# A diffusion backbone step on one core: negated weight copies put directly behind their rounding, dots spread differently

## The chip, the cores and the metric

The kernel runs on one core of one Trainium2 chip. The metric is the device time of one execution in microseconds. The engines are named as the profile names them: PE (matrix engine, PEld its weight loads), DVE (vector engine), ACT (scalar engine), POOL (GpSimd, here a queue that issues transfers), SP (a queue that issues most of the loads).

## What is computed

The reference is one inference step of a backbone of two layers over T = 640 tokens (512 latent ones and 128 of context) of D = 1024 features, in float32. Layer 0 mixes tokens by a bidirectional state-space scan, layer 1 by differential attention; after each mixer stands a gated convolutional channel mixer (called FFN below). Each part is normalised, shifted, scaled and gated by a linear map of a conditioning vector:

```python
def modulation(cvec, w, b):
    m = jax.nn.silu(cvec) @ w + b
    return jnp.split(m[:, None, :], 6, axis=-1)

def conv_ffn(h, up_w, conv_w, conv_b, down_w):
    u = dwconv(h @ up_w, conv_w, conv_b)
    a, v = jnp.split(u, 2, axis=-1)
    return (jax.nn.silu(a) * v) @ down_w
...
        xp = xp + p_g1 * op
        xs = xs + s_g1 * os_
        ffn_p = (ffn_up_w[i], ffn_conv_w[i], ffn_conv_b[i], ffn_down_w[i])
        xp = xp + p_g2 * conv_ffn(modulate(xp, norm_ffn_g[i], p_sh2, p_sc2), *ffn_p)
        xs = xs + s_g2 * conv_ffn(modulate(xs, norm_ffn_g[i], s_sh2, s_sc2), *ffn_p)
```

The hidden width of the FFN is 2816, that is 22 tiles of 128 rows in each of its two halves.

## The kernel before

Every large product is made of three products of rounded numbers: a matrix is split into a rounded high part and a low part, the rest, and hi·hi, hi·lo and lo·hi are added up. So each weight needs a high tile `whi` and a low tile `wlo`. Weights come in numbered *units*: `prefetch` (L157) has SP load `raw<u>`, up to 512 KB (128 x 1024), and `cast` (L169) makes whi and wlo. There are three ways: most units have whi copied by ACT and wlo subtracted by DVE; units whose `kind` is a tuple are sums of two weights, `s0` to `s3`, made by DVE, copied by ACT and subtracted by DVE; and units in the set `summed` (nearly all loads of the up weights that need no sum) get a second ACT copy with the sign turned, minus the rounded weight, after which POOL issues a transfer that adds the weight from memory into wlo (L202 to L204). The last way takes no DVE time, but the low part is there only when the transfer has landed.

An FFN (L695) takes the 22 tiles of the hidden width in pairs: tile p of one half with tile p of the other. The first pairs (6 in layer 0, 4 in layer 1, `S0`) are two plain tiles each. The others (`pair8`, L794) are computed with seven block products in place of eight. A block is 12 matmuls into one bank; X, V and Y are the banks of one pair. X is written by the first block (`begin7`, L779), copied out by ACT as `uraw`, and then gets more blocks on top; V is copied out as `p5`. Four units belong to a pair: wa, two of sums, and wv; in the layer-0 FFN, units 77 to 80 belong to pair 6, the first of the kind, 81 to 84 to the next. What ends a pair is `epilogue` (L712): a convolution of both halves on ACT and DVE (tiles `ca` and `cv`), their gated product cv, its rounded copy `mh` and its low part `ml`, made like wlo with a negated copy and a POOL transfer.

The pairs go in five groups (`SUB`): after a group, `project_out` (L344) multiplies the finished tiles by down weights into tiles `po`; ACT copies these out as `y`, and a POOL transfer adds y to the residual in memory (`xd`). The last group of six goes through `project_last` (L359), which adds to the residual in SBUF (`xr`) and takes the squares for the next norm.

Beside this runs a task that computes layer 1's modulation, `mod_rest` (L660). It has 48 tiles; each is a load of 512 KB (`mw`, issued by SP, two buffers) and two DVE instructions of 128 x 1024 (L674, the *dots*), outputs `junk` and mw. A task is advanced by `hook`, called after every second step of matmuls; `self.gap` says how many hooks pass from a dot to the next, and each dot is held until the matmul issued last before it has run. Which tiles are done where is set by `DOTS = 3, 36, 48`: tiles 0 to 2 in layer 0's mixer output (there the loads are called `ew`), 3 to 35 in layer 0's FFN, 36 to 47 in the attention.

The order on each engine's queue is made by a scheduler from data dependences and priorities, roughly the order of the program; what stands in `tc.high_priority()` is put ahead of what does not. In `pair8` the copies `uraw` and `p5` and the additions to uraw stand in it.

Of the kernel before, what the change touches and what calls it, by code (L numbers as in the profile page):

```python
# [11 lines left out]
BF16 = mybir.dt.bfloat16  # L12
I32 = mybir.dt.int32
AF = mybir.ActivationFunctionType
ALU = mybir.AluOpType
# [21 lines left out]
SUB = (0, 4), (4, 8), (8, 12), (12, 16), (16, 22)  # L37
# [3 lines left out]
RAW = 4  # L41
NS = 4
S0 = 6, 4
DOTS = 3, 36, 48
TH = T // 2
ATT_SPLIT = 6
NF = 11
# [3 lines left out]
class Step:  # L51
# [117 lines left out]
    def cast(self, upto):  # L169
        while len(self.wcast) <= min(upto, len(self.units) - 1):  # L170
            u = len(self.wcast)
            self.prefetch(u)
            n = self.units[u][1]
            r = self.wraw[u]
            kind = self.units[u][2]
            place = self.units[u][3] or ("x" if self.px and u % 5 > 2 else "w")
            wp, t, b = (self.pw, "w", 3) if place == "w" else (self.px, "x", 2)
            hi = wp.tile([P, 1024], F32R, tag=t + "hi", name=f"whi{u}", bufs=b)
            lo = wp.tile([P, 1024], F32R, tag=t + "lo", name=f"wlo{u}", bufs=b) if u else None
            if u == 0:  # L180
                half = lambda t, j: t.rearrange("p (k j m) -> p k j m", k=KT, j=2)[:, :, j, :]
                r3 = r[:, :n].rearrange("p (k m) -> p k m", k=KT)
                self.act(half(hi, 0), r3, AF.Copy)
                self.tt(half(hi, 1), r3, half(hi, 0).bitcast(F32), ALU.subtract)
            elif isinstance(kind, tuple):
                ns, j0, ia, iv = kind
                self.prefetch(u + iv)
                ra, rv = self.wraw[u + ia], self.wraw[u + iv]
                w = ns * P
                for j in range(j0, j0 + 1024 // w):  # L190
                    x = self.slot("f", f"s{j}", bufs=NF)[:, :w]
                    a, b, op = ((rv[:, :w], rv[:, w:2 * w], ALU.add), (self.s.get(0), ra[:, :w], ALU.subtract),
                                (ra[:, :w], rv[:, :w], ALU.subtract), (ra[:, w:2 * w], self.s.get(1), ALU.subtract))[j]
                    self.tt(x, a, b, op)
                    self.s[j] = x
                    c = slice(w * (j - j0), w * (j - j0 + 1))
                    self.act(hi[:, c], x, AF.Copy)
                    self.tt(lo[:, c], x, hi[:, c].bitcast(F32), ALU.subtract)
            else:
                c = slice(kind or 0, n)  # L200
                self.act(hi[:, c], r[:, c], AF.Copy)
                if u in self.summed:  # L202
                    self.act(lo[:, c], r[:, c], AF.Copy, scale=-1.0)
                    self.nc.gpsimd.dma_start(lo[:, c], self.units[u][0][:, c], accum_op=ALU.add)  # L204
                else:
                    self.tt(lo[:, c], r[:, c], hi[:, c].bitcast(F32), ALU.subtract)
            self.wcast[u] = (hi, lo)

# [486 lines left out]
    def ffn(self, l, h, nextnorm, pool):  # L695
# [3 lines left out]
        mid = {}  # L699
# [131 lines left out]
        def pair(p, more):  # L831
            if p >= S0[l]:
                if p == S0[l]:
                    self.drain(self.seven)
                    finish_operands()
                return pair8(p, more)
            ua = copy_out(self.next_tile(h, "up"))
            epilogue(p, ua, copy_out(self.next_tile(h, "up")))

        self.start_tiles(h)  # L840
        done = 0
# [6 lines left out]
        with self.tc.tile_pool(name=f"sums{l}", bufs=1, side="right", reuse_waits="tile") as tp:  # L848
            self.seven = self.add(operands(sevens, tp), 1)
            for s, (k0, k1) in enumerate(SUB):  # L850
                while done < min(k1 + 1, FT):
                    if not l and done == 3:
                        junk = lambda: self.slot("sq", "junk", BF16, cols=1024, bufs=1)
                        self.modtask = self.add(self.mod_rest(1, *DOTS[:2], self.cb, self.mod_row, junk), 1)
                    self.gap, self.rest = 3 if done < S0[0] else 9, 0
                    pair(done, done + 1 < min(k1 + 1, FT))
                    done += 1
                if s < len(SUB) - 1:
                    self.gap = 4
                    if self.modtask:  # L860
                        self.modtask[1] = self.ticks + 1
                    self.project_out(mid, range(k0, k1), self.gate(l, 1),
                                     to=lambda i: self.slot("y", "y", bufs=3, pool=pool) if l
                                     else self.slot("f", "y", bufs=NF) if i % 2 else self.tmp("y"))
# [1 line left out]
            self.drain(self.modtask)  # L866
            self.modtask = None
        self.restore()
        self.project_last(mid, range(*SUB[-1]), self.gate(l, 1), nextnorm, parts="CD" if l else "AB", save=not l)


    def ssd_consts(self, pool):
# [266 lines left out]
    def ssd(self, h, dtps, nextnorm, pool):  # L1139
        xf = [[None] * 4 for _ in range(4)]  # L1140
        zs = [[] for _ in range(4)]
        bcs, scanned, gt = [None] * 4, [False] * 4, [None] * 4

        def finish(g):

            yield from self.ssd_group(g, xf[g], *bcs[g], pool)
            scanned[g] = True
            while len(zs[g]) < 4:
                yield 1
            for t in range(4):  # L1150
                self.stt(xf[g][t], xf[g][t], 0.5, zs[g][t], ALU.mult, ALU.mult)
            yield 1
            yield from self.ssd_norm(g, xf[g], pool)

        def z_tiles(g):
            for t in range(4):
                ps = self.next_tile(h, "z")
                z = self.slot("f", f"z{g}{t}", bufs=NF)
                self.act(z, ps[:, PO:PO + T], AF.Tanh, scale=0.5)
                self.stt(z, z, 1.0, ps[:, PO:PO + T], ALU.add, ALU.mult)  # L1160
                zs[g].append(z)

        tmod = self.add(self.mod_rows(1, pool, 7))
        tdt = self.add(self.ssd_dt(dtps))
        self._advance(tdt)
        for g in range(4):
            for t in range(4):
                ps = self.next_tile(h, "x")
                xf[g][t] = self.xslot(f"xf{g}{t}") if g < 2 else self.slot("f", f"xf{g}{t}", bufs=NF)
                self.ssd_xbc(ps, 4 * g + t, xf[g][t])  # L1170
            bc = []
            for j in (16, 20):
                ps = self.next_tile(h, "bc")
                o = self.slot("bc", f"bc{g}{j}", bufs=3, pool=pool)
                self.ssd_xbc(ps, j + g, o)
                bc.append(o)
            if g == 0:
                self.drain(tmod)
                self.drain(tdt)
            else:  # L1180
                z_tiles(g - 1)
                while not scanned[g - 1]:
                    self._advance(gt[g - 1])
            bcs[g] = bc
            gt[g] = self.add(finish(g), 2)
        z_tiles(3)
        self.drain(gt[0])
        self.drain(gt[1])
        hy = [self.split(xf[i // 4][i % 4], f"y{i}") for i in range(8)]
        self.x = []  # L1190
        for i in range(KT):
            xi = self.xslot(f"xr{i}")
            self.nc.sync.dma_start(xi, self.a["xT"][i])
            self.x.append(xi)
        self.project_out(hy, range(8), self.gate(0, 0))
        self.drain(gt[2])
        self.drain(gt[3])
        hy = [self.split(xf[2 + i // 4][i % 4], f"y{8 + i}") for i in range(8)]
        self.modtask = self.add(self.mod_rows(2, pool, 7))
        row = lambda: pool.tile([P, 1024], F32, tag="rb", name="ew", bufs=3)  # L1200
        junk = lambda: self.slot("t", "junk", BF16, cols=1024, bufs=4)
        self.gap, self.rest = 4, 3
        early = self.add(self.mod_rest(1, 0, DOTS[0], self.cond_rows(row), row, junk), 8)
        self.project_last(hy, range(8), self.gate(0, 0), nextnorm, save=True, before=[early])


# [199 lines left out]
    def heads(self, h, nextnorm, pool):  # L1406
# [7 lines left out]
        next(consts, None)  # L1414
        junk = lambda: pool.tile([P, 1024], BF16, tag="junk", name="junk", bufs=1)
        self.gap, self.rest = 6, 0
        dots = self.add(self.mod_rest(1, *DOTS[1:], self.cb, self.mod_row, junk), 10)
        for hd in range(8):
            q, qp = self.att_evac(self.next_tile(h, "q"), hd, "q", pool)
            k, kp = self.att_evac(self.next_tile(h, "k"), hd, "k", pool)  # L1420
# [36 lines left out]
    def weight_units(self):  # L1457
# [9 lines left out]
        def ffn(l):  # L1467
# [13 lines left out]
            return out  # L1481

        u = [(*x, None, None) for x in u] + ffn(0)
        v, u = u, []
        for hd in range(8):
# [155 lines left out]
```

## Time and profile before

| | us |
|---|---|
| median of 3 runs | 1855.98 (1850.47 to 1857.3) |
| the profiled execution | 1847.69 |
| its span, first to last instruction | 1845.9 |
| PE busy | 1782.4 (97%) |
| DVE busy | 1465.1 (79%) |
| ACT busy | 1166.3 (63%) |
| POOL busy | 153.4 (8%) |

Times in rows are counted from the span's start. Layer 0's FFN lies at about 567 to 1018, with its first seven-product pair at 676 and projections near 725, 804, 884 and from 985 on; the attention begins after it, and layer 1's FFN lies in the stretch 1400 to 1780. A row of an engine's timeline has the start, the duration, the engine, the line, the operation, out<-in, the shape, and in brackets how long the engine had been idle and what ended that. A row of PE's waits has the total, how often, and the longest.

### The profile page before, as it was taken

The numbers are of one execution on the slowest core, as the hardware profiler recorded it, in microseconds if no ns is written. First come the engines' busy times: TensorE is split into PE (matmuls) and PEld (weight loads), VectorE is DVE, ScalarE is ACT, GpSimd is POOL, SyncE is SP. The second block draws the span as 40 slices with busy tenths as digits, with TensorE's granted clock in tenths as the row PEclk, the third lists the DMA queues.
The fourth block names the chain that finished last, engine by engine and source line by source line (L and its number), as shares of the span: only waits on it lengthen the run. The fifth ranks groups of instructions, "written<-read, shape, count | busy, mean of one in ns | idle before, by whom it ended". The sixth has DMA issues, their size and how long they took to land.

```text
span 1845.9 us, 33794 instructions
## 1 busy us (share of the span) xinstructions
PE 1782.4 (97%) x12914; PEld 1684.1 (91%) x12914; DVE 1465.1 (79%) x2907; ACT 1166.3 (63%) x2329; POOL 153.4 (8%) x180
## 2 busy tenths in 40 slices
PE   7999999999999999999999989999999999999996
PEld 5899999999989999999999888888899999999996
DVE  5689999999858968879776788888878856758584
ACT  3489686879426656667574556566636666767661
POOL 0000000000000121212210000000000122122210
PEclk9999999999999999999999999999999999999998
DMA  9844353446655697988966222223134587787871
GB/s 344 259 133 139 99 148 105 120 142 196 213 178 160 168 239 175 228 214 190 233 154 217 88 85 82 88 83 113 48 126 116 120 167 176 155 182 157 173 196 58
DMA packets 116990, 289.13 MB, mean 157 GB/s; under 512 B 13422, under 2 KB 20186, under 8 KB 116828
## 3 DMA queue, kind: packets, MB, share of 16 engines
q1 hardware_dynamic: 90908, 223.92, 37.2%
q0 software_dynamic: 25344, 62.53, 19.9%
q8 instruction: 101, 1.65, 0.4%
q10 hardware_dynamic: 576, 0.52, 0.1%
q14 instruction: 61, 0.50, 0.1%
HBM read 238.36 MB, written 34.80 MB: 148 GB/s over the span
## 4 chain that ended last, share of the span: by engine, by line
PE 41%; DVE 9%; issue 7%; DMA 4%; ACT 2%; POOL 1%; DVEq 0%; POOLq 0%; ACTq 0%
PE up L112 15%; PE po L112 15%; DMA wlo<-in_w_up 3%; PE k L112 2%; PE st L112 2%; PE q L112 2%; DMA ml<-cv 1%; PE ov L112 1%; PE sl L112 1%; PE v L112 1%; ACT e L103 1%; PE wt L1375 1%; DVE sm L1309 1%; DVE wlo L109 1%; DVE w L106 1%
## 5 line engine op out<-in xcount | busy, mean ns | idle before, releaser
L103 ACT ACTIVATE whi<-raw 128x1024 fp32r<-128x1024 f32 (+2 forms) x259 | 225.9, 872 | 196.2 <-PE po L112 120.2
L109 DVE TENSOR_TENSOR wlo<-raw,whi 128x1024 fp32r<-128x1024 f32 (+3 forms) x188 | 188.1, 1004 | 45.4 <-ACT whi L103 42.8
L112 PE MATMUL po<-ml,whi 128*128 128x256 f32 (+1 forms) x704 | 165.9, 309 | 2.6 <-DMA ml<-cv 2.5
L112 PE MATMUL po<-mh,whi 128*128 128x256 f32 (+1 forms) x704 | 165.8, 309 | 0.2 <-ACT mh L103 0.2
L204 POOL DMA_DIRECT2D wlo<-in_w_up x70 | 62.0, 885 | 1243.5 <-PE st L112 1022.8
L112 PE MATMUL po<-mh,wlo 128*128 128x256 f32 (+1 forms) x704 | 165.3, 308 | 0.0
L109 DVE TENSOR_TENSOR wlo<-s,whi 128x512 fp32r<-128x512 f32 x136 | 92.0, 687 | 60.7 <-ACT whi L103 60.2
L112 PEld LDWEIGHTS po<-ml,whi 128*128 128x128 f32 x704 | 127.5, 188 | 3.6 <-DMA ml<-cv 3.4
L112 PE MATMUL up<-Th,whi 128*128 128x320 f32 x408 | 127.1, 312 | 3.6 <-ACT uraw L103 3.6
L112 PEld LDWEIGHTS po<-mh,whi 128*128 128x128 f32 x704 | 127.4, 188 | 0.8 <-ACT mh L103 0.5
L112 PEld LDWEIGHTS po<-mh,wlo 128*128 128x128 f32 x704 | 127.8, 188 | 0.0
L112 PE MATMUL up<-Th,wlo 128*128 128x320 f32 x408 | 127.0, 311 | 0.0
L112 PE MATMUL up<-Tl,whi 128*128 128x320 f32 x408 | 126.7, 311 | 0.0
L112 PE MATMUL up<-h01h,wlo 128*128 128x320 f32 (+2 forms) x400 | 113.6, 313 | 8.2 <-DMA wlo<-in_w_up 8.2
L103 ACT ACTIVATE whi<-s 128x512 fp32r<-128x512 f32 x136 | 84.2, 627 | 53.8 <-DVE s L109 34.9
L112 PE MATMUL up<-h01h,whi 128*128 128x320 f32 (+2 forms) x400 | 112.6, 311 | 0.0
L112 PE MATMUL up<-h01l,whi 128*128 128x320 f32 (+2 forms) x400 | 112.5, 311 | 0.0
L112 PE MATMUL up<-h11h,wlo 128*128 128x320 f32 (+1 forms) x368 | 107.2, 309 | 1.5 <-DMA wlo<-in_w_up 1.5
L112 PE MATMUL up<-h11l,whi 128*128 128x320 f32 (+1 forms) x368 | 107.0, 308 | 0.0
L112 PE MATMUL up<-h11h,whi 128*128 128x320 f32 (+1 forms) x368 | 107.0, 308 | 0.0
L106 DVE SCALAR_TENSOR_TENSOR cv<-uraw,fcw,cv 128x511 f32<-128x511 f32 (+1 forms) x176 | 85.3, 546 | 26.3 <-ACT cv L103 26.3
L106 DVE SCALAR_TENSOR_TENSOR ca<-uraw,fcw,ca 128x511 f32<-128x511 f32 (+1 forms) x176 | 86.7, 546 | 9.9 <-ACT ca L103 7.9
(528 smaller groups left out, 5373.7 us busy)
## 6 DMA issues: line engine op xcount, KB each, us to landing
raw<-in_w_up SPq DMA_DIRECT2D x88, 512.0 KB, 3.8
mw<-in_modT SPq DMA_DIRECT2D x45, 512.0 KB, 5.7
raw<-in_w_in SPq DMA_DIRECT2D x40, 512.0 KB, 6.2
rb<-rowd SPq DMA_DIRECT2D x40, 512.0 KB, 5.6
xd<-y POOLq DMA_DIRECT2D x64, 320.0 KB, 7.2
wlo<-in_w_up POOLq DMA_DIRECT2D x36, 512.0 KB, 6.4
raw<-in_w_dn SPq DMA_DIRECT2D x64, 256.0 KB, 3.2
ml<-cv POOLq DMA_DIRECT2D x42, 320.0 KB, 4.2
```

The lines of the kernel that those rows point to most:

```text
L103: return self.nc.scalar.activation(out, in_, func, **k)
L106: return self.nc.vector.scalar_tensor_tensor(out, in0, s, in1, op0, op1)
L109: return self.nc.vector.tensor_tensor(out, a, b, op)
L112: self.last = self.nc.tensor.matmul(out, lhsT, rhs, start=start, stop=stop, skip_group_check=more)
L204: self.nc.gpsimd.dma_start(lo[:, c], self.units[u][0][:, c], accum_op=ALU.add)
L1309: nc.vector.tensor_reduce(st[:, m:m + 1], s, AX.X, ALU.max, negate=True)
L1375: nc.tensor.transpose(pm[:, b * P:(b + 1) * P], ws[b][:, kc * P:(kc + 1) * P], self.ident)
```

## The change

Three things change, and with the scheduler they move rows on all queues. First, for units in `summed`, the rounded copy, the negated copy and the POOL transfer are put into `high_priority`. Second, `DOTS` becomes 4, 32, 36, 48: four tiles instead of three in layer 0's mixer output, with gaps of 3 and 5 hooks for 4 and 7 and a shorter first wait; tiles 4 to 31 in the FFN of layer 0; 32 to 35 in its last projection, as a task that `project_last` drains ahead of its last three tiles; the attention's twelve stay. Third, the gaps in layer 0's FFN change: 3 hooks up to the fifth pair, 16 in the sixth and seventh, then 11 (before: 3 for six pairs, then 9); in projections 4 for the first and 5 for later ones (before: 4).

```diff
--- before.py
+++ after.py
@@ -41,7 +41,7 @@
 RAW = 4
 NS = 4
 S0 = 6, 4
-DOTS = 3, 36, 48
+DOTS = 4, 32, 36, 48
 TH = T // 2
 ATT_SPLIT = 6
 NF = 11
@@ -198,11 +198,13 @@
                     self.tt(lo[:, c], x, hi[:, c].bitcast(F32), ALU.subtract)
             else:
                 c = slice(kind or 0, n)
-                self.act(hi[:, c], r[:, c], AF.Copy)
                 if u in self.summed:
-                    self.act(lo[:, c], r[:, c], AF.Copy, scale=-1.0)
-                    self.nc.gpsimd.dma_start(lo[:, c], self.units[u][0][:, c], accum_op=ALU.add)
+                    with self.tc.high_priority():
+                        self.act(hi[:, c], r[:, c], AF.Copy)
+                        self.act(lo[:, c], r[:, c], AF.Copy, scale=-1.0)
+                        self.nc.gpsimd.dma_start(lo[:, c], self.units[u][0][:, c], accum_op=ALU.add)
                 else:
+                    self.act(hi[:, c], r[:, c], AF.Copy)
                     self.tt(lo[:, c], r[:, c], hi[:, c].bitcast(F32), ALU.subtract)
             self.wcast[u] = (hi, lo)
 
@@ -852,11 +854,11 @@
                     if not l and done == 3:
                         junk = lambda: self.slot("sq", "junk", BF16, cols=1024, bufs=1)
                         self.modtask = self.add(self.mod_rest(1, *DOTS[:2], self.cb, self.mod_row, junk), 1)
-                    self.gap, self.rest = 3 if done < S0[0] else 9, 0
+                    self.gap, self.rest = (3 if done < S0[0] - 1 else 16 if done < S0[0] + 1 else 11), 0
                     pair(done, done + 1 < min(k1 + 1, FT))
                     done += 1
                 if s < len(SUB) - 1:
-                    self.gap = 4
+                    self.gap = 5 if s else 4
                     if self.modtask:
                         self.modtask[1] = self.ticks + 1
                     self.project_out(mid, range(k0, k1), self.gate(l, 1),
@@ -866,7 +868,13 @@
             self.drain(self.modtask)
             self.modtask = None
         self.restore()
-        self.project_last(mid, range(*SUB[-1]), self.gate(l, 1), nextnorm, parts="CD" if l else "AB", save=not l)
+        more = []
+        if not l:
+            self.gap = 3
+            junk = lambda: self.slot("t", "junk", BF16, cols=1024, bufs=4)
+            more = [self.add(self.mod_rest(1, *DOTS[1:3], self.cb, self.mod_row, junk), 1)]
+        self.project_last(mid, range(*SUB[-1]), self.gate(l, 1), nextnorm, parts="CD" if l else "AB", save=not l,
+                          before=more)
 
 
     def ssd_consts(self, pool):
@@ -1199,8 +1207,8 @@
         self.modtask = self.add(self.mod_rows(2, pool, 7))
         row = lambda: pool.tile([P, 1024], F32, tag="rb", name="ew", bufs=3)
         junk = lambda: self.slot("t", "junk", BF16, cols=1024, bufs=4)
-        self.gap, self.rest = 4, 3
-        early = self.add(self.mod_rest(1, 0, DOTS[0], self.cond_rows(row), row, junk), 8)
+        self.gap, self.rest = 3, 2
+        early = self.add(self.mod_rest(1, 0, DOTS[0], self.cond_rows(row), row, junk), 4)
         self.project_last(hy, range(8), self.gate(0, 0), nextnorm, save=True, before=[early])
 
 
@@ -1414,7 +1422,7 @@
         next(consts, None)
         junk = lambda: pool.tile([P, 1024], BF16, tag="junk", name="junk", bufs=1)
         self.gap, self.rest = 6, 0
-        dots = self.add(self.mod_rest(1, *DOTS[1:], self.cb, self.mod_row, junk), 10)
+        dots = self.add(self.mod_rest(1, *DOTS[2:], self.cb, self.mod_row, junk), 10)
         for hd in range(8):
             q, qp = self.att_evac(self.next_tile(h, "q"), hd, "q", pool)
             k, kp = self.att_evac(self.next_tile(h, "k"), hd, "k", pool)
```

On DVE, ahead of the first seven-product pair, before the change and after it (`junk` and `mw` are the two outputs of a dot, `s0` the first sum of the pair, from unit 80's load; `wlo78` its low part; `ca` the convolution of the pair before):

```order
L674 ISA junk_7973,mod1_116<-mw_7894,cb_7015 128x1024
L674 ISA mod1_116 128x1
L674 ISA mw_7894,mod1_116<-mw_7894,cb_7016 128x1024
L674 ISA mod1_116 128x1
L674 ISA junk_8014,mod1_116<-mw_7971,cb_7015 128x1024
L674 ISA mod1_116 128x1
L109 TENSOR_TENSOR s0_8031<-raw80_8027 128x512
L109 TENSOR_TENSOR s1_8035<-s0_8031,raw77_7882 128x512
L106 SCALAR_TENSOR_TENSOR ca_8096<-uraw_8022,fcw0_6751,ca_8096 128x511
L109 TENSOR_TENSOR wlo78_8030<-s0_8031,whi78_8029 128x512
```

```order
L676 ISA junk_7978,mod1_116<-mw_7899,cb_7020 128x1024
L676 ISA mod1_116 128x1
L109 TENSOR_TENSOR s0_8031<-raw80_8027 128x512
L109 TENSOR_TENSOR s1_8035<-s0_8031,raw77_7887 128x512
L109 TENSOR_TENSOR wlo78_8030<-s0_8031,whi78_8029 128x512
L106 SCALAR_TENSOR_TENSOR ca_8090<-uraw_8022,fcw0_6756,ca_8090 128x511
L109 TENSOR_TENSOR wlo78_8030<-s1_8035,whi78_8029 128x512
```

Ahead of s0 stand 21 dots of the FFN before and 19 after, so the last dot ahead of it reads an earlier tile of mw; of the three dots between s0 and the pair's gated product before (rows further on), one is left.

On ACT at the same pair, before and after (the `uraw` with 128x320 is the copy of X, the one with 128x256 and 128x384 that of a plain tile; `mh5` and `ml5` belong to the plain pair before; units 79 and 80 are the pair's second sums and its wv):

```order
L103 ACTIVATE cv_8102<-uraw_8093,fcw0_6751 128x640
L103 ACTIVATE mh5_8110<-cv_8102 128x640
L103 ACTIVATE uraw_8137<-up_8139 128x320
L103 ACTIVATE p5_8160<-up_8140 128x320
L103 ACTIVATE ml5_8111<-cv_8102 128x640
L103 ACTIVATE whi79_8127<-s2_8129 128x512
L103 ACTIVATE whi79_8127<-s3_8133 128x512
L103 ACTIVATE whi80_8155<-raw80_8027 128x512
L103 ACTIVATE uraw_8137<-up_8139 128x320
L103 ACTIVATE wlo80_8156<-raw80_8027 128x512
```

```order
L103 ACTIVATE uraw_8087<-up_8026 128x384
L103 ACTIVATE whi79_8121<-s2_8123 128x512
L103 ACTIVATE whi80_8150<-raw80_8027 128x512
L103 ACTIVATE cv_8096<-uraw_8087,fcw0_6756 128x640
L103 ACTIVATE uraw_8131<-up_8133 128x320
L103 ACTIVATE wlo80_8151<-raw80_8027 128x512
L103 ACTIVATE whi79_8121<-s3_8127 128x512
L103 ACTIVATE p5_8155<-up_8134 128x320
L103 ACTIVATE uraw_8131<-up_8133 128x320
L103 ACTIVATE mh5_8104<-cv_8096 128x640
```

mh5 stood ahead of X's copy and now stands behind both copies of X; the copies of units 79 and 80 have moved ahead of, or between, the copies of the banks.

On POOL where the fourth group's projection ends and the last group begins (units 148 and 149 are the wv of the group's first pair and the wa of the next one; xd are the additions of y), before and after:

```order
L357 DMA xd5_6150<-y_10685 128x640
L357 DMA xd6_6151<-y_10721 128x640
L357 DMA xd7_6152<-y_10764 128x640
L204 DMA wlo148_10802<-in_w_up 128x512
L204 DMA wlo149_10821<-in_w_up 128x1024
L204 DMA wlo153_10971<-in_w_up 128x1024
```

```order
L359 DMA xd5_6154<-y_10656 128x640
L359 DMA xd6_6155<-y_10695 128x640
L205 DMA wlo149_10798<-in_w_up 128x1024
L359 DMA xd7_6156<-y_10739 128x640
L205 DMA wlo148_10777<-in_w_up 128x512
L205 DMA wlo153_10949<-in_w_up 128x1024
```

Unit 149's transfer has moved ahead of xd7 and of unit 148's. In the seven-product pairs of the second FFN, ACT's negated copy of the next wa moves likewise from behind X's copy to directly behind its rounding.

## The prediction

> **What bounds the kernel now.** I read the span of the core first, then the engine shares, then windows of the matrix engine (PE) around each place where the chain of waits leaves it, then the waits of PE in the two channel mixers, and last the rows of the engines that release it.
>
> ```profile
> core 0: 1845.9 us, clock 0.992
> PE 1782.4 (97%) x12914; PEld 1684.1 (91%) x12914; DVE 1465.1 (79%) x2907; ACT 1166.3 (63%) x2329; POOL 153.4 (8%) x180
> ```
>
> PE is busy 97% of the span, and the change leaves its matmuls alone, so it can only win what PE loses in the stretches it touches. Each window row below gives start and end, length, PE busy with the count of matmuls, granted clock, DMA share, GB/s.
>
> ```profile
> 683.00:693.00 10.00, 6.44 (x27) 0.66 0.55 148
> 695.00:699.00 4.00, 2.75 (x17) 1.00 1.07 223
> 723.00:728.00 5.00, 3.06 (x21) 1.00 0.85 223
> 763.00:767.00 4.00, 3.38 (x23) 1.00 0.65 218
> 804.00:807.00 3.00, 2.39 (x16) 1.00 0.95 277
> 843.00:847.00 4.00, 2.26 (x16) 1.00 1.05 342
> 867.00:871.00 4.00, 3.35 (x23) 1.00 0.56 104
> 922.00:935.00 13.00, 9.28 (x53) 0.87 0.55 119
> 1449.00:1453.00 4.00, 2.75 (x18) 1.00 0.51 100
> 1461.00:1464.00 3.00, 2.73 (x19) 1.00 1.06 257
> 1466.00:1777.00 311.00, 311.00 (x2128) 1.00 0.78 169
> ```
>
> The last row is the second channel mixer running without a stall: 311/2128 = 0.146 us a matmul. Length less 0.146 times the count is what each window loses: 6.05, 1.52, 1.93, 0.64, 0.66, 1.66, 0.64 and 5.25 in the first channel mixer (18.35 together), 1.37 and 0.22 in the second: 19.9 us. What PE waited for there, first mixer (three rows: total, times, longest), then the second (one row):
>
> ```profile
> PE up L112 <- DMA wlo<-in_w_up: 8.2, 6, 3.7
> PE up L112 <- ACT uraw L103: 3.6, 1, 3.6
> PE po L112 <- DMA ml<-cv: 2.5, 2, 1.9
> PE up L112 <- DMA wlo<-in_w_up: 1.5, 2, 1.3
> ```
>
> These are 14.3 + 1.5 us of waiting; the remaining four are matmuls at a lower clock and short gaps. Two waits are long:
>
> ```profile
> 686.65 0.63 PE L112 MATMUL up<-Th,whi 128*128 128x320 f32 x1 [3.56 <-ACT uraw L103]
> 926.86 0.41 PE L112 MATMUL up<-h01h,wlo 128*128 128x320 f32 x1 [3.73 <-DMA wlo<-in_w_up]
> ```
>
> The first is the first seven-product pair (the "first block product"), losing 6.05 with 3.56 of it waiting: the other 2.49 is matmuls after it, in the window whose granted clock is 0.66. The second is 3.73 of 5.25, clock 0.87; after the waits of up to 1.9 us the windows show 1.00. [...]
>
> **The change, part by part.** *Dots thinned before the first block product.* Vector engine (DVE) and scalar engine (ACT) rows there:
>
> ```profile
> 672.25 1.23 DVE L674 CUSTOM_DVE_ANT_0 junk<-mw,cb 128x1024 bf16<-128x1024 f32 x1 [3.32 <-DMA mw<-in_modT]
> 673.40 0.69 DVE L109 TENSOR_TENSOR s<-raw 128x512 f32<-128x512 f32 x1
> 684.68 0.82 DVE L109 TENSOR_TENSOR cv<-ca,cv 128x640 f32<-128x640 f32 x1
> 685.53 0.74 ACT L103 ACTIVATE mh<-cv 128x640 fp32r<-128x640 f32 x1 [3.32 <-DVE cv L109]
> 686.17 0.42 ACT L103 ACTIVATE uraw<-up 128x320 f32<-128x320 f32 x1
>   DMA mw<-in_modT: 19.4, 7
> L674 DVE CUSTOM_DVE_ANT_0 junk<-mw,cb x45: 1203/1219/1229, 614.4 to 1270.8; 128x1024 bf16<-128x1024 f32 x45
> ```
>
> The sum s0 stands in DVE's row behind a dot that waited 3.32 us for its 512 KB tile; from s0 to the gated product cv DVE needs 11.3 us, of which three dots are 3 x 1.22 = 3.7; ACT stands at mh, which waits for cv, with the evacuation uraw (the one PE waits for) behind it. In the changed order two dots fewer stand ahead of s0 (19 for 21), so the tile that it waits for is one load earlier, mh stands behind the evacuation, and one dot is left in the stretch. PE loses its filler too: it no longer takes blocks of later units ahead. I follow the natural order on PE: the two plain tiles, X, V, then X again. At 12 matmuls x 0.146 = 1.76 us a block the second X comes about 3.5 us after the first starts, and the evacuation needs before it the two copies and the convolution's first step (about 0.6 + 0.6 + 0.9 from rows of such shapes), then 0.42 itself: 2.5 us. It fits by 1 us. The window at 695, where a low part came late, hangs on the same chain. Of 6.05 + 1.52 = 7.6 I take 7.0; ends 0 (stall stays) and 7.6.
>
> *Negated copies and their transfers directly behind the rounding.* Scalar-engine and GpSimd-queue (POOL) rows of the long wait at 926:
>
> ```profile
> 912.07 1.06 ACT L103 ACTIVATE whi<-raw 128x1024 fp32r<-128x1024 f32 x1 [1.48 <-issue]
> 916.19 1.60 ACT L103 ACTIVATE wlo<-raw 128x512 fp32r<-128x512 f32 x2
> 917.19 1.83 POOL L204 DMA_DIRECT2D wlo<-in_w_up  x2 [1.87 <-ACT wlo L103]
> 755.95 0.89 POOL L204 DMA_DIRECT2D wlo<-in_w_up  x1 [1.52 <-PE up L112]
> DMA to landing us min/median/max: 4.7/6.3/15.0
> 726.00:764.00 38.00, 37.36 (x254) 37.36 (x255) 26.99 (x45) 21.74 (x46) 9.60 (x11) 1.00 0.99 263
> mw<-in_modT SPq DMA_DIRECT2D x5, 512.0 KB, 9.4
> ```
>
> The rounded copy of unit 149 ends at 913.1, its negated copy starts near 916.7 as second of two, and its transfer is the second of the two that POOL issues from 917.19, so about 918.1; it lands when PE goes on at 926.86, 8.7 later. Behind the rounding, the negated copy ends near 914.1 and the transfer goes out near 914.2, some 3.9 earlier, ahead of xd7 and of unit 148's: at the same 8.7 it lands at 922.9, when PE wants it (926.86 - 3.73 = 923.1). Of 5.25 I take 4.0 (ends 0 and 5.25), since transfers collide. At 763 and 843 the last transfer (units 100 and 124, at 755.95 for the first) already goes out right behind its copy; it gains only because units 101 and 125 go out one place earlier and fewer tiles for dots are loaded: 726 to 764 is full (share 0.99, 263 GB/s), and one 512 KB load fewer is 2.0 us of it. Of 0.64 + 1.66 I take 1.5. At 867 unit 133's negated copy stood behind four other steps of ACT (two roundings, an evacuation, ca: 0.4 to 0.9 each by the rows quoted last); now directly behind the rounding: 0.6 of 0.64. The second mixer loses no dots, only the copies and transfers move: 1.0 of 1.6.
>
> *Fewer loads in the two waits for ml* (723, 804: 1.93 + 0.66). Their place in POOL's queue stays; between units 81 and 92 SP loads 4 tiles where it loaded 7, so 1.5 MB less at 263 GB/s, 6 us of transfer. I take 1.8 of 2.6; ends 0 and 2.6.
>
> *What it costs.* The number of dots is unchanged (3 + 33 + 12 = 4 + 28 + 4 + 12 = 48 tiles of two). Four of the tiles now stand in the first mixer's last projection: a dot ahead of the last low part there can delay it, the others lie beside gate additions where DVE waits on PE.
>
> ```profile
> 986.19 0.82 DVE L109 TENSOR_TENSOR ml<-cv,mh 128x640 fp32r<-128x640 f32 x1 [0.81 <-ACT mh L103]
> 1001.08 1.14 DVE L106 SCALAR_TENSOR_TENSOR xr<-po,mod,xr 128x256 f32<-128x256 f32 x3 [2.44 <-PE po L112]
> 581.16 0.85 ACT L103 ACTIVATE uraw<-st 128x384 f32<-128x384 f32 x2
> ```
>
> I take 0.7 for it, between 0 and one pair of dots, 2.4. At the mixer's start three copies go ahead of the evacuation at 581.16: 0.4, between 0 and 3 x 1.06. The fourth early tile costs two dots in the first layer's mixer output, with DVE partly idle: 0, hidden by PE's own work; 2.4 if that cover were gone.
>
> Sum: 7.0 + 4.0 + 1.5 + 0.6 + 1.0 + 1.8 - 0.7 - 0.4 = 14.8 us. Against the profiled execution, 1847.69 us (span 1845.9 and 1.8 around it), that is 1832.9, a ratio of 0.9920. That execution is 0.45% below the median of the runs, 1855.98 (1850.47 to 1857.3), so the median should come to 1841. About 0.5%, 9.3 us, is what can be told from no change.
>
> **Rivals.**
>
> *Reordering alone: transfers land as late as before.* With the DMA engines at 0.99 from 726 to 764, whatever goes out earlier only pushes another back. Then the waits at unit starts in both mixers stay (4.0 + 1.5 + 1.0 not won): 8.3, so 1848, just within 0.5%. For it speaks that full window and the landing of up to 15.0 us; against it that 867 and 922 lose with a share of 0.56 and 0.55. [...]
>
> *The first block product still stalls.* If the dot ahead of s0 waits for its tile as now (19.4 us in seven such waits), s0 comes at 673 again and PE has lost its filler: 7.0 not won, 7.8 in all, 1848.
>
> *Slower: the evacuation waits behind the negated copy.* In each of 34 seven-product pairs (16 and 18) the full negated copy now stands ahead of X's evacuation. ACT in the second mixer now:
>
> ```profile
> 1503.87 0.62 ACT L103 ACTIVATE whi<-s 128x512 fp32r<-128x512 f32 x1
> 1504.39 0.91 ACT L103 ACTIVATE ca<-uraw,fcw 128x640 f32<-128x640 f32 x1
> 1505.20 0.41 ACT L103 ACTIVATE uraw<-up 128x320 f32<-128x320 f32 x1
> 1505.52 1.05 ACT L103 ACTIVATE wlo<-raw 128x1024 fp32r<-128x1024 f32 x1
> ```
>
> PE has one block between X's two uses, 1.76 us, less the 0.41: 1.3 us of cover. If a delay past that cover reached 0.44 us a pair it would eat the 14.8; the copy's whole 1.05 would cost 34 x 1.05 = 35.7, so 20.9 net: 1877. Against it: the copy (0.95 from start to start) replaces a rounding and ca ahead of uraw, 1503.87 to 1505.20 = 1.33, so the evacuation should come earlier, not later.
>
> **How the numbers follow.** The sum as worked out 0.54 (1841, its own range 1836 to 1846), reordering alone 0.17, the stall that stays 0.18, the slower one 0.08, and 0.03 that both middle ones hold together (1.3 won, 1855). Both middle rivals lie at 1848, near the bound of 1846.7, so a third of their chance counts as faster: faster 0.66; same 0.26; slower 0.08. All losses back at no cost would be 1847.69 - 19.9, by the ratio 1836; with the runs' own scatter of some 4 us the range begins at 1832. Upward it takes in the middle rivals and the scatter: 1853.
>
> **What would show it.** Right: no PE wait on uraw near 680, PE's window of ten us there at clock 1.00; unit 149's transfer issued near 914 and no wait over 1 us at its unit's start; ml and wlo waits under 4 us in the first mixer where they were 10.7; no new gap at 986. Wrong: a PE wait on ACT uraw in many pairs of the second mixer (the slower rival); the same wait lengths with earlier issues (reordering); s0 again at 673 (the stall).

## The result

| | before | after |
|---|---|---|
| median of 6 runs, us | 1856.64 (1850.47 to 1859.28) | 1842.92 (1840.27 to 1846.63) |
| profiled execution, us | 1847.69 | 1841.11 |

The ratio is 0.9934, 95% interval 0.9913 to 0.9955: 0.66% faster, where 0.80% was forecast. The profiled executions differ by less than the medians, 6.6 us against 13.7, since the one of before lies 9 below its median and below all of the timed runs in the table; where about a third of that may come from is seen below.

The same views of the changed kernel, core and engines first, then PE's waits in the first channel mixer (FFN), then in the second:

```profile
core 0: 1839.3 us, clock 0.994
PE 1778.6 (97%) x12914; PEld 1680.3 (91%) x12914; DVE 1462.4 (80%) x2907; ACT 1168.7 (64%) x2329; POOL 153.4 (8%) x180
```

```profile
PE up L112 <- DMA wlo<-in_w_up: 3.4, 3, 2.7
PE po L112 <- DMA ml<-cv: 3.1, 2, 2.2
...
PE up L112 <- ACT uraw L103: 0.5, 1, 0.5
```

```profile
PE up L112 <- ACT uraw L103: 2.5, 1, 2.5
PE up L112 <- DVE uraw L109: 2.0, 1, 2.0
PE up L112 <- DMA wlo<-in_w_up: 0.2, 1, 0.2
```

In the first mixer the waits on wlo, uraw and ml came to 14.3 us and come to 7.0. In the second they were 1.5 and are 4.7. All these kernels issue the same 12914 matmuls, so the time from the start of the n-th to that of the m-th tells where PE loses. The last column is (m - n) x 0.1462, the pace without stalls (not worked out for the last projection); "copies" and "dots" are the two halves of the change alone, of which more below:

| matmuls, us | place | before | after | copies | dots | no stall |
|---|---|---|---|---|---|---|
| 4600 to 5100 | plain pairs, first projection | 73.2 | 76.4 | 78.0 | 73.2 | 73.1 |
| 5100 to 5300 | first seven-product pair | 38.0 | 30.1 | 40.0 | 29.6 | 29.2 |
| 5300 to 5950 | groups 2 and 3 | 99.4 | 95.6 | 103.7 | 95.7 | 95.0 |
| 5950 to 6500 | groups 3 and 4 | 83.8 | 81.3 | 84.6 | 82.8 | 80.4 |
| 6500 to 6850 | start of the last group | 57.1 | 54.2 | 52.0 | 56.1 | 51.2 |
| 6850 to 7300 | last projection | 64.9 | 65.8 | 65.0 | 65.2 | – |
| 10200 to 10400 | second mixer, first seven-product pair | 31.4 | 34.8 | 36.7 | 36.2 | 29.2 |

The first seven-product pair gave back 7.9 of the 8.8 us it lost. DVE and then ACT of the changed kernel there:

```profile
667.32 1.23 DVE L676 CUSTOM_DVE_ANT_0 junk<-mw,cb 128x1024 bf16<-128x1024 f32 x1 [2.65 <-DMA mw<-in_modT]
668.47 0.69 DVE L109 TENSOR_TENSOR s<-raw 128x512 f32<-128x512 f32 x1
685.77 0.82 DVE L109 TENSOR_TENSOR cv<-ca,cv 128x640 f32<-128x640 f32 x1
```

```profile
683.66 0.44 ACT L103 ACTIVATE uraw<-up 128x320 f32<-128x320 f32 x1 [1.07 <-PE up L112]
```

s0 starts at 668.5 (673.4 before), though the dot ahead of it still waits 2.65 us for its tile, and the evacuation at 683.66 waits for PE's block only; the gated product cv comes at 685.8, later than before, and no wait of PE follows from it.

At the last group's start the transfers go out earlier as planned, and PE still waits 2.69 us. POOL, PE, the transfer of 256 KB (unit 148's) with its time from issue to landing, and a window over the time in which the transfers are under way:

```profile
903.65 0.87 POOL L205 DMA_DIRECT2D wlo<-in_w_up  x1 [2.63 <-ACT wlo L103]
907.36 0.88 POOL L205 DMA_DIRECT2D wlo<-in_w_up  x1 [1.52 <-ACT uraw L103]
```

```profile
916.93 0.42 PE L112 MATMUL up<-h01h,wlo 128*128 128x320 f32 x1 [2.69 <-DMA wlo<-in_w_up]
```

```profile
wlo<-in_w_up POOLq DMA_DIRECT2D x1, 256.0 KB, 9.5
```

```profile
895.00:917.00 22.00, 19.31 (x132) 18.92 (x130) 14.25 (x24) 15.00 (x28) 5.23 (x6) 1.00 0.97 230
```

and the same transfer and window of the kernel before:

```profile
wlo<-in_w_up POOLq DMA_DIRECT2D x1, 256.0 KB, 6.4
```

```profile
904.00:927.00 23.00, 19.27 (x132) 19.01 (x131) 16.72 (x28) 14.29 (x27) 4.51 (x6) 1.00 1.03 262
```

Unit 149's transfer is issued at 903.65 now, ahead of unit 148's at 907.36; unit 148's, half the size, lands 9.5 later (6.4 before), and PE waits for that one. The DMA engines are at a share of 0.97 (1.03 before) up to the landing. The prediction read a share of 0.55 for this place, from a window that begins 1 us before PE's wait and reaches 8 us beyond its end, when the transfers are nearly done or landed.

Two losses are new. At the first mixer's start, ACT (changed kernel):

```profile
580.89 2.01 ACT L103 ACTIVATE whi<-raw 128x1024 fp32r<-128x1024 f32 x2 [1.52 <-issue]
582.80 1.99 ACT L103 ACTIVATE wlo<-raw 128x1024 fp32r<-128x1024 f32 x2
584.70 0.85 ACT L103 ACTIVATE uraw<-st 128x384 f32<-128x384 f32 x2
594.20 0.73 ACT L103 ACTIVATE mh<-cv 128x640 fp32r<-128x640 f32 x1
```

and before, DVE and PE of the changed kernel following:

```profile
588.80 0.73 ACT L103 ACTIVATE mh<-cv 128x640 fp32r<-128x640 f32 x1
```

```profile
604.82 0.82 DVE L109 TENSOR_TENSOR f<-h01h,h01l 128x640 f32<-128x640 f32 x1 [2.95 <-DMA ml<-cv]
```

```profile
639.93 0.56 PE L112 MATMUL po<-ml,whi 128*128 128x256 f32 x2 [2.18 <-DMA ml<-cv]
```

Four copies of weights in a row, of two units, push the first evacuations from 581.16 to 584.70; two more units are copied ahead of mh, which moves from 588.80 to 594.20. (Of each, 0.7 us is that the changed kernel begins this mixer later.) The transfer of ml0 lands that much later, DVE's operand sums wait for the buffer that it reads (until 604.82, before 598.24), and 35 us on, PE waits 2.18 us for the low part of a product.

In the second mixer, at the first seven-product pair, ACT (with one row from further on) and DVE of the changed kernel:

```profile
1444.35 0.63 ACT L103 ACTIVATE whi<-s 128x512 fp32r<-128x512 f32 x1 [1.45 <-DVE s L109]
1444.89 0.61 ACT L103 ACTIVATE whi<-raw 128x512 fp32r<-128x512 f32 x1
1445.41 0.61 ACT L103 ACTIVATE wlo<-raw 128x512 fp32r<-128x512 f32 x1
1445.93 0.42 ACT L103 ACTIVATE uraw<-up 128x320 f32<-128x320 f32 x1
1452.95 0.63 ACT L103 ACTIVATE whi<-raw 128x512 fp32r<-128x512 f32 x1 [3.53 <-DMA raw<-in_w_dn]
```

```profile
1453.62 0.69 DVE L109 TENSOR_TENSOR wlo<-raw,whi 128x512 fp32r<-128x512 f32 x1 [3.47 <-ACT whi L103]
1454.22 0.48 DVE L109 TENSOR_TENSOR uraw<-up,uraw 128x320 f32<-128x320 f32 x1
```

X's evacuation now stands behind three copies of weights, the first of which waits for DVE's s2; and PE waits for it, 2.5 us. This is the prediction's slower rival, in one pair and not in 34. The second wait there, 2.0 us on DVE's addition to uraw, has another cause: the addition stands on DVE behind a low part that waits 3.47 us for its rounding, and the rounding on ACT waited 3.53 us for the load of a down weight.

### The profile page after: what moved, and what is told of

Read it like the earlier page. It is cut to its first block, busy times and chain, and to the rows that moved or that the text cites. A ratio compares the mean times of both kernels' runs of the same rounds, so it can differ in the third digit from the quotient of the medians.

```text
span 1839.3 us, 33771 instructions
## 1 busy us (share of the span) xinstructions
PE 1778.6 (97%) x12914; PEld 1680.3 (91%) x12914; DVE 1462.4 (80%) x2907; ACT 1168.7 (64%) x2329; POOL 153.4 (8%) x180
## 5 line engine op out<-in xcount | busy, mean ns | idle before, releaser
L106 DVE SCALAR_TENSOR_TENSOR cv<-uraw,fcw,cv 128x127 f32<-128x127 f32 (+1 forms) x176 | 85.7, 544 | 6.6 <-ACT cv L103 6.6
```

The source lines that it names most:

```text
L106: return self.nc.vector.scalar_tensor_tensor(out, in0, s, in1, op0, op1)
```

## The experiments

Each was timed against the kernel before on the same chip. Ratios are to before, with 95% intervals.

**Copies alone.** The first hunk of the change, DOTS and gaps as before.

> The kernel before, with only the negated copies and their transfers directly behind the rounding; the dots stand as before. Theory (each part wins its own waits): PE's wait on uraw near 683 stays at 3 us or more with its slow stretch, and so do the waits for ml at 724 and 805; the wait at the last group's start (3.7 us at 923) goes under 1.5 us; the second channel mixer loses about 3 us against before, as the changed kernel does. About 1852 to 1857 where before is 1856. Rival (the transfers do it all, the dots nothing): the gain of the whole change, 1841 to 1845.

1862.01 against 1856.37, ratio 1.0033 (1.0017 to 1.0049): slower. DVE, then PE's waits in the first mixer:

```profile
680.65 0.69 DVE L109 TENSOR_TENSOR s<-raw 128x512 f32<-128x512 f32 x1
```

```profile
PE po L112 <- DMA ml<-cv: 10.8, 5, 3.8
PE up L112 <- ACT uraw L103: 6.5, 2, 5.8
PE up L112 <- DMA wlo<-in_w_up: 2.0, 4, 1.2
```

The theory's waits are there, larger than expected: s0 comes 7.2 us later than before (680.65 against 673.40), the wait on uraw is 5.8, and ml costs 10.8 where it was 2.5. The wlo waits fell from 8.2 to 2.0, so the copies do win what they are put earlier for, and lose more elsewhere. The rival is out: they are not what made the changed kernel faster.

**Dots alone.** The change without its first hunk.

> The changed kernel with the copies and transfers put back to where they were; only the dots are thinned and four tiles moved. Theory: the wait on uraw near 683 is gone (under 0.6 us) and the waits for ml at 724 and 805 too, some 8 to 9 us; the waits for wlo at 764, 844, 923 stay at about 0.6, 1.7 and 3.7, and the second channel mixer is as before. About 1846 to 1849 where before is 1856. Rival (the transfers do it all): no gain, 1855 to 1857.

1841.31, ratio 0.9924 (0.9899 to 0.9948): the gain of the whole change, more than expected. The largest of PE's waits in the first mixer, then in the second:

```profile
PE up L112 <- DMA wlo<-in_w_up: 5.7, 3, 3.2
```

```profile
PE up L112 <- DMA wlo<-in_w_up: 5.1, 3, 3.1
```

uraw and ml are gone from the first mixer, the three waits at the groups' starts stay (0.5, 2.1, 3.2). The second mixer loses 5.1 on wlo with the copies where they were before, so the 1.5 of the profile before need not be the usual state of that code. Matmuls 10200 to 10400 took 36.2, 34.5, 32.0, 35.2, 32.4, 34.8 and 34.9 us in the seven profiles of kernels below whose second mixer has the old code, mean 34.3, and 31.4 in the profile before: that may account for about 3 of the 9 us by which the profiled execution lies under its median. These are seven different kernels; whether executions of the kernel before spread in the same way was not tried. The new code took 34.8 and 36.7.

**The new place in the first mixer alone.** `if u in self.summed and u < 190:` for the three instructions in `high_priority`, the old order otherwise.

> The changed kernel with the new place of copies and transfers in layer 0's channel mixer alone. Theory (the second mixer's waits of 2.5 us on ACT's uraw and 2.0 us on DVE's uraw near 1444 and 1453 come from the copies of units 214 to 218 standing ahead): both waits go, the two of before (1.3 and 0.3 for wlo) come back, so 3 to 4 us faster than the changed kernel: about 1839. Rival (they come from layer 0's side or from transfers): the two waits stay, 1843.

1841.19, ratio 0.9920 (0.9897 to 0.9944). PE's waits in the second mixer:

```profile
PE up L112 <- DMA wlo<-in_w_up: 3.7, 3, 1.9
PE po L112 <- DMA ml<-cv: 1.8, 1, 1.8
```

The waits on uraw are gone and those on wlo are back, as the theory has it, but at 3.7 us and not 1.6, so the second mixer is even: the copies there change what PE waits for. So the theory's 3 to 4 us did not come; the time can't be told from the changed kernel's.

**And there only from unit 67 on.**

```diff
-                if u in self.summed and u < 190:
+                if u in self.summed and 66 < u < 190:
```

> As the one with the new place in layer 0's mixer alone, and there only from the pairs behind the plain ones on (units 67 and up), so that ml0's transfer goes out ahead of those of units 64 and 65 again. Theory (the wait of 2.2 us for ml at 637 comes from ml0's transfer landing late, which holds back DVE's operand sums that need its buffer): DVE's wait for the ml transfer near 600 goes from 3.0 back to 1.7 us or less and PE's wait at 637 under 0.5: 2 us less than the one with the new place in all of layer 0's mixer. Rival (the wait at 637 comes from the dots ahead of the gated product): it stays at about 2 us.

1838.19, ratio 0.9908 (0.9887 to 0.9928). The wait at 637 (2.4 with all of the first mixer) is gone, and matmuls 4600 to 5100 take 73.2 us again, not 76.4. The medians lie 3.0 us apart where 2 were expected, but their intervals overlap. So the cause of that wait is the new place of the units up to 66; the run puts back their copies and their transfers together, and only the rows above, with ACT's copies ahead of the first evacuations and of mh, speak for the copies.

**Loads off.** The kernel before; in the first mixer one tile is loaded and all dots read it.

```diff
-            if t < t1 - 1:
+            if t < t1 - 1 and (t0 != DOTS[0] or t < t0):
                 nxt = alloc()
                 nc.sync.dma_start(nxt, a["modT"][t + 1])
...
-                i = nc.vector.tensor_tensor_reduce(w if c else junk, w, cb[c], ...
+                i = nc.vector.tensor_tensor_reduce(w if c and t0 != DOTS[0] else junk, w, cb[c], ...
```

> The kernel before, with the loads of the dots' tiles in layer 0's channel mixer left out but for the first: every dot there reads that one tile, so that part of the modulation is not computed; DVE's time for dots stays whole. It tells whether the dots cost by their transfers or by DVE's time. Theory (both: a dot that waits for its tile holds s0 back, and the loads crowd the other transfers): no wait of DVE for a tile, s0 of the first seven-product pair near 668, PE's wait on uraw under 1 us, waits for ml and wlo in layer 0's mixer together under 4 us where they were 10.7: 1842 to 1846 where before is 1856. Rival (DVE's time for the dots alone makes the waits): waits as before, 1853 to 1857.

1850.63 against 1854.20, ratio 0.9978 (0.9965 to 0.9992). DVE and PE's waits:

```profile
669.35 0.69 DVE L109 TENSOR_TENSOR s<-raw 128x512 f32<-128x512 f32 x1
```

```profile
PE up L112 <- DMA wlo<-in_w_up: 7.2, 3, 3.9
PE po L112 <- DMA ml<-cv: 3.5, 3, 2.0
```

s0 comes 4 us earlier and the wait on uraw is gone, 6.3 us of the first seven-product pair (31.7 for 38.0). Three whole dots still stand between s0 and the gated product here, so taking away the first link alone, the dot that waits for its tile, takes the wait away. The waits for wlo and ml stay, so the dots' loads are not what crowds those transfers: here the theory fell, and the time with it (1842 to 1846 expected).

**Dots short.** The kernel before, loads kept; in the first mixer the dots take 64 of 1024 columns.

```diff
-                i = nc.vector.tensor_tensor_reduce(w if c else junk, w, cb[c], ...
+                n = 64 if t0 == DOTS[0] else 1024
+                i = nc.vector.tensor_tensor_reduce((w if c else junk)[:, :n], w[:, :n], cb[c][:, :n], ...
```

> The kernel before, with every load of a tile kept, but the dots in layer 0's channel mixer taken over 64 columns of 1024, so that part of the modulation is not computed: the transfers stay, DVE's time for 66 dots (about 1.1 us each, 73 us of DVE) goes. Theory (both count): PE's wait on uraw near 683 goes under 1 us, since three dots fewer hold the gated product back, and the waits for ml go, since the products come earlier; the waits for wlo at the groups' starts stay (6 to 8 us together): 1845 to 1849. Rival (transfers alone make the waits): 1853 to 1857.

1837.65, ratio 0.9912 (0.9890 to 0.9935), 7 us below the range expected. DVE, then PE's waits in the first mixer:

```profile
667.21 0.69 DVE L109 TENSOR_TENSOR s<-raw 128x512 f32<-128x512 f32 x1
```

```profile
PE up L112 <- DMA wlo<-in_w_up: 6.6, 3, 3.4
PE po L112 <- DMA ml<-cv: 1.0, 1, 1.0
```

With DVE's time gone the wait on uraw goes (first pair 29.4) and ml falls to 1.0; wlo stays. So ml hangs on DVE's time, wlo neither on that nor on the loads. For uraw this run takes both links at once: the dot ahead of s0 no longer waits for its tile (s0 is at 667.21), and those behind s0 are short. What the dots between s0 and the gated product cost by themselves was not separated.

**Four tiles back.** Dots alone, but DOTS = 4, 36, 36, 48 and no task in the last projection.

> The kernel with only the dots changed, less one step: the four tiles stay in layer 0's channel mixer instead of its last projection (the four early tiles and the new gaps are kept), so what is left of them is done in one go ahead of that projection. Theory (the gain comes from thinning around the first block product): the gain of the dots alone stays up to the last group, and the dots in one go cost at most 8 x 1.22 = 10 us of DVE there, of which PE sees 0 to 5: 1841 to 1846. Rival (moving four tiles out is what wins, by loads): 1849 to 1856, with the waits for wlo at 832 and 910 back above 2 us and 4 us.

1844.08 against 1854.20, ratio 0.9938 (0.9922 to 0.9954). PE's waits in the first mixer:

```profile
PE up L112 <- DMA wlo<-in_w_up: 6.0, 4, 3.4
PE po L112 <- DMA ml<-cv: 3.4, 1, 3.4
```

The gain up to the last group stays; what comes back is one wait of 3.4 us for ml in the last projection, which takes 69.9 us for 65.2 with the dots alone. By the medians, moving the four tiles is worth about 3 us of the gain; the intervals of the two ratios overlap.

**Fewer transfers at the starts.** The kernel with the new place from unit 67 to 189, and

```diff
-        self.summed = (set(up) - set(up[:5]) - set(up[half:half + 5]) - after)
+        self.summed = (set(up) - set(up[:5]) - set(up[half:half + 5]) - after - {100, 124, 148, 215, 218})
```

> As the one with the new place from unit 67 on in layer 0's mixer, and the low parts of the units for which PE waits at the groups' starts (100, 124, 148, and 215 and 218 in the second mixer) are subtracted by DVE, without negated copy and transfer. Theory (these waits are transfers in a full set of DMA engines, so only fewer transfers, not earlier ones, take them away): the waits for wlo at 755, 834, 912 and 1437 (0.7, 0.4, 1.6 and 2.0 us) go, four DVE subtractions of 0.7 and one of 1.0 us are hidden: 1833 to 1836. Rival (DVE is as late there): DVE's low part is waited for instead, 1838 to 1841.

1831.09 against 1854.20, ratio 0.9869 (0.9854 to 0.9883): beyond what was expected. No wait for wlo is left in the first mixer (the waits of PE there, the two longest):

```profile
PE ms L112 <- ACT sq L103: 2.9, 1, 2.9
PE up L112 <- ACT uraw L103: 0.9, 1, 0.9
```

**Copies alone, from unit 67 to 189.** The kernel before with the new place for these units.

> The kernel before with the new place of copies and transfers only in layer 0's channel mixer and there from unit 67 on; dots as before. Theory (the copies alone made the kernel slower because the transfers of units 64 and 65 went ahead of ml0's, whose late landing held DVE back some 6 us up to s0 of the first seven-product pair): ml0's transfer goes out first again, s0 comes at 673 to 675 instead of 680.7, PE's wait on uraw falls from 5.8 to about 3.6 us, the wait at 637 from 2.6 to 0; about 6 us less than the copies alone: 1853 to 1857 where before is 1856. Rival (the loss comes from the copies ahead of evacuations in the seven-product pairs): still 1859 to 1863.

1858.79 against 1855.97, ratio 1.0025 (1.0013 to 1.0037). DVE and PE's waits:

```profile
673.65 0.69 DVE L109 TENSOR_TENSOR s<-raw 128x512 f32<-128x512 f32 x1
679.18 1.23 DVE L680 CUSTOM_DVE_ANT_0 junk<-mw,cb 128x1024 bf16<-128x1024 f32 x1 [1.10 <-DMA mw<-in_modT]
```

```profile
PE po L112 <- DMA ml<-cv: 7.0, 3, 3.5
PE up L112 <- ACT uraw L103: 5.7, 2, 5.4
```

Half of what was expected: 2.8 us are lost against before, where the copies alone lose 5.6. s0 is back at 673.65 and the wait at 637 gone, as expected, but the wait on uraw is 5.4 and ml 7.0. The gated product now waits behind a dot that waits 1.1 for its tile; why ml is later by 4.5 us in all was not settled. By the profiles the loss of copies alone has thus two parts, of which the start is one; by the times the two runs can't be told apart.

**Fewer transfers, old place of copies.** Dots alone with the same five units taken out of `summed`.

> The dots changed, the copies and transfers where they stood before, and the low parts of units 100, 124, 148, 215 and 218 subtracted by DVE. Theory (the new place of copies wins nothing that fewer transfers do not win): 1830 to 1834, as the kernel with both. Rival (the new place wins its own 3 us): 1834 to 1838.

1830.95 against 1855.97, ratio 0.9892 (0.9862 to 0.9921): like the one with the new place. The waits for wlo at 755 and 834 are gone, one of 2.8 us on unit 149 at 906 stays; with the new place that one goes too (no wait for wlo above), so the copies win that wait, but the medians, 0.14 us apart, show no gain.

**Fewer transfers in the kernel before.** The same five units only.

> The kernel before, with only the low parts of units 100, 124, 148, 215 and 218 subtracted by DVE. Theory (the waits at the groups' starts depend on nothing but these transfers; the first seven-product pair and the ml waits on DVE): the waits for wlo at 764, 844, 926 go, 6 to 8 us with those of the second mixer; the wait on uraw stays at 3.6: 1847 to 1850 where before is 1856. Rival (with all 33 tiles of dots DVE has no time for them): PE waits for DVE's low part there instead, 1853 to 1858.

1848.41 against 1855.97, ratio 0.9970 (0.9954 to 0.9985). As expected in time; the waits on uraw (3.7) and ml (4.7) stay, and so do waits on wlo of 2.2 at the first pair and 3.4 on unit 149. That last one was expected to go and did not: with unit 148's transfer taken away, the wait for unit 149's is 3.4 us where it was 3.7. So a transfer less took away the wait for its own unit's low part, and left nearly all of the wait for the next one.

**And unit 149.** The one with fewer transfers and the old place, 149 added to the five.

> As the kernel with the dots changed, the old place of copies, and five low parts by DVE, and unit 149's low part by DVE as well; it is the only long wait for a transfer left in layer 0's mixer (2.8 us at 906). Theory (only a transfer taken away takes its wait away): that wait goes, DVE's subtraction of 1.0 us is hidden, about 2.5 to 3 us less: 1827 to 1830. Rival (DVE is as late there, since the last pair of low parts comes in a row): PE waits for DVE's low part instead, 1830 to 1833.

1829.95 against 1855.00, ratio 0.9856 (0.9829 to 0.9883). The wait at 906 is gone. Its median is the lowest of all, 13 us under the changed kernel's, with the copies in their old place; from the other two with fewer transfers and thinned dots its interval does not tell it apart.

## Why the prediction was right, and where its steps were not

The time was right (1841 forecast, 1842.9 measured), and so was the main mechanism, the dots. That the number came so close is in part luck. Of the 14.8 us, 7.1 were booked on the new place of copies and transfers (4.0 + 1.5 + 0.6 + 1.0, the 1.5 in part on fewer loads), which on balance gave nothing that can be told: 0.9934 with them, 0.9924 with the dots alone. The dots gave what was missing: in the table, matmuls 4600 to 7300 take 13.8 us less with the dots alone, where the prediction had booked 7.0 + 1.8 - 0.7 for them. Of the signs named ahead, PE's wait on uraw near 680 fell to 0.5 us; ml and wlo came to 6.5 us together and not under 4, and a wait of 2.7 us stayed at the last group's start. The 7.0 and the 4.0 count the matmuls at a lower clock behind the two long waits (2.49 and 1.52 us) as won along with the waits. That was the author's estimate: both places show a clock of 1.00 after the change (683 to 693 and 914 to 924, waits of 0.5 and 2.69 us), but the last section has 0.83 around waits of 1.9 us and 1.00 around waits of 3.4, so no run shows that the shorter wait gave them back.

- *Dots thinned before the first block product, 7.0*: right in size and mechanism. 7.9 came back, 8.4 with the dots alone. Loads off takes the wait away with the first link named alone, the dot that waits for its tile ahead of s0; the second, the dots between s0 and the gated product, was only taken away together with the first.
- *Fewer loads in the two waits for ml, 1.8*: both waits went, but not by loads. With the loads off they stay (2.0 and 0.9); with DVE's time off they go. This step named the wrong cause, DMA for DVE.
- *Negated copies and transfers behind the rounding, 4.0 + 1.5 + 0.6*: the step that failed, as a gain of its own. Alone they win the wlo waits (8.2 to 2.0) and make the kernel 5.6 us slower. In the changed kernel the last group's start gave 2.9 of 4.0, of which 1.0 comes with the dots alone; the wait, 3.73, is still 2.69 and has passed to unit 148. About half of the 2.9 is that no slow stretch followed that wait (clock 1.00 from 914 to 924, where the prediction's window showed 0.87), which the last section shows not to be a matter of the wait's length. The 1.5 for units 100 and 124 did come: these two waits fell from 2.4 to 0.7 us, and the dots alone leave them at 2.5. The rival "reordering alone" describes the last group's start better, and the DMA share that spoke against it was read from the wrong window. What took a wait away in every run where it was tried is a low part made by DVE and not by a transfer (those at 755, 834 and 906). Unit 133's wait went with the dots alone too.
- *Second mixer, 1.0*: wrong in size: the profile shows 3.4 us lost. Against the seven profiles with the old code it is even. The base of 1.6 was one execution; in matmuls 10200 to 10400 it lost 2.2 us against the pace, the other seven 2.8 to 7.0.
- *Mixer's start, cost 0.4*: mis-sized. It is 3.2 us: mh came 5.4 us later, and the cost fell on a wait some 50 us on, not on the evacuations themselves.
- *Last projection, cost 0.7*: 0.9 (64.9 to 65.8). Four tiles back shows that leaving them costs more.
- *The slower rival*: it happened in one pair, not in 34; in the others the negated copy replaced more work ahead of the evacuation than it added, as was read: at the pair of the prediction's rows the evacuation now comes 1.89 us after the rounding of wa begins (1493.78 to 1495.67), before 2.28 (1502.92 to 1505.20).
- *The median by the ratio*: the profiled pair moved 6.6 us, the medians 13.7. The sum, 14.8, was built on an execution that had lost less than usual in the second mixer, where the change was expected to win little; had the copies' terms been left out, the rest, 7.0 + 1.8 - 0.7 - 0.4, is 7.7 and gives 1848, too high.

## What to carry to other kernels

Putting work ahead on a queue was paid here by what stood there (mh 5.4 us later): look for the buffer and the engine that wait for the displaced step, and follow them until PE, which here was some 50 us later. Judge whether an earlier transfer lands earlier by the DMA share while it is under way (here 0.97, with 9.5 us to landing for unit 148's where it was 6.4), not by the share while its reader waits (0.55 in the prediction's window); where the share is that high, try to make the awaited tile on an engine with time to spare instead (here DVE, and no wait for wlo was left in the first mixer). And before a stall of a microsecond or two is booked as a gain, look whether other executions with the same code have it.

## What the runs showed of the hardware

The clock after a wait did not follow the wait's length. PE's windows of ten us around waits of 3.35 us (four tiles back), 3.37 (dots short), 1.89 (loads off) and 1.94 (new place in the first mixer alone), in this order:

```profile
907.50:917.50 10.00, 6.65 (x46) 1.00 0.54 131
```

```profile
829.00:839.00 10.00, 6.63 (x46) 1.00 0.73 203
```

```profile
836.00:846.00 10.00, 8.11 (x45) 0.83 0.68 163
```

```profile
1439.50:1449.50 10.00, 8.06 (x45) 0.83 0.28 61
```

The two longer waits left the clock whole and the two shorter ones lowered it. So what the prediction's windows showed, 0.66 and 0.87 with the waits of 3.56 and 3.73 us and 1.00 with those of up to 1.9, held only for the waits it had seen. In each of the two windows at 0.83, 10 us less 45 matmuls of 0.146 us and less the wait leaves 1.5 us that the lowered clock cost, most of the wait over again. PE's rows of the kernel before show such matmuls: behind the wait of 3.73 us, six matmuls from 927.11 to 927.84 start 0.146 us apart, twelve from 928.04 to 930.97 start 0.27 apart, and from 931.43 on it is 0.146 again. What decides it was not tried.
